# A decoder block on one core: the expert stage gathers its tokens by f32 products from a residual kept in the weights' column order, adds its results into a second buffer, and has four more weight tiles

## The chip, the cores and the metric

One NeuronCore of a Trainium2 chip runs the whole program. The metric is the device time in microseconds of one execution. TensorE (PE) multiplies matrices, with its weight loads (PEld) shown apart; VectorE (DVE), ScalarE (ACT) and GpSimd (POOL) work elementwise; the sync engine (SP) issues the large DMAs, which 16 DMA engines carry out. All engines run side by side and wait for each other by semaphores.

## The reference

A decoder block over 512 tokens of 2048 columns, all in f32: an attention half (two head groups, of which nothing is touched here), the output projection with a residual, and then a mixture of 32 experts in four groups. Cut to what matters:

```python
mix = jnp.concatenate([o_nsa, o_gla], axis=-1)
x = x + g1 * (mix @ w_out[l])
h = _rmsnorm(x, norm2_w[l]) * (1.0 + sc2) + sh2
# group = argmax(h @ w_rg + b_rg); inside it the two experts of the largest logits (h @ w_re + b_re)
# expert e on its tokens xb: (silu(xb @ w_gate[e]) * (xb @ w_up[e])) @ w_down[e], weighted, added up
x = x + g2 * _moe(h, w_rg, b_rg, w_re, b_re, w_gate, w_up, w_down)
return _rmsnorm(x, norm_f_w)
```

Each expert has 12 MB of weights (gate and up 2048 x 512, down 512 x 2048), and all 32 are read once, whichever tokens they get: 403 MB of the 580 MB that the program reads.

## The kernel before, in words

The program is written as one function that records instructions; a scheduling layer puts them on the engines' queues, and makes an instruction wait when a tile's buffer is still read or written by an earlier user. `tc.issue_after` pins an instruction behind another one. A tile name such as `raw` is a ring of buffers: a DMA into the next one waits until its last reader is through.

*Output projection* (loop over n, four column chunks of 512, and q, four groups of rows). `mhi` and `mlo` are the mixer's output, split in two fp32r parts (fp32r is a format whose product takes one pass), held in the buffers `hi0..3` and `lo0..3` of the pool `big`. `wo_products` multiplies; L947 and L948 scale the sum by g1 and add x, which gives the residual `x1`; L950 sums its squares. Transposes of `x1` times `wr2` give the router's logits along the way (L975-978, and for the last chunk L958-969).

*Routing.* The weights of the norm follow as `r2`; `h2_chunk(n)` writes `x1` times `r2` in two fp32r parts, `h2h` and `h2l`, into `hi{n}` and `lo{n}`, with its columns reordered: the experts' gate and up weights are loaded so that a partition p holds four neighbouring rows 4p to 4p+3, and the reordering makes every 128 columns match one of these rows. `WARM` matmuls on TensorE stand ahead of the routing's first counting products (L1057). `onehot` builds `G`, a 0/1 matrix from tokens to the slots of a block of experts.

*Expert stage.* Twelve blocks of 128 slots: the first has experts 0 and 1 (64 slots each); then, sorted by their token count, three experts (64 + 32 + 32) or two (64 + 64) in the order 3, 3, 2, 3, 3, 2, 3, 3, 2, 3, 3. A block's steps, each pinned behind the one before by `then`:

- `gather(n, i)`: for each column chunk n, `G` times `h2h` and `h2l` over four token tiles, eight products into one PSUM bank; ACT copies the bank to `xe`
- `turn(n)`: four transposes of `xe`; ACT scales and shifts them by the second norm into `xt`
- `gate_up(n, which)`: each expert's columns of `xt` times its 1 MB weight tile; experts sit in different column groups of the array and run at the same time
- `weights`, `turn_up`, and `down(hf, kk)`: the scatter matrix, the transposed activation, the down product
- `scatter(n, i)`: the results, split in two, times the scatter matrix, added to `x1` by DVE (L1253)

`run_block` interleaves them: gather n+1 stands between the two halves of `gate_up` of n, the last two chunks of the previous block's scatter between the gathers. `wtile` hands out the weight tiles of 1 MB: four `raw`, three `raw2`, and once, for tiles 8 and 9, two sets of small buffers that are still free (`early`). All weight tiles are issued by SP in this order. The end norms `x1` and stores it.

Of the kernel before, what the change touches and what calls it, by code (L numbers as in the profile page):

```python
# [8 lines left out]
F32 = mybir.dt.float32  # L9
# [22 lines left out]
WARM = 6  # L32
# [6 lines left out]
def block_kernel(ctx, tc, a, out, dbg=None, stop=None):  # L39
# [823 lines left out]
    mp = RS.enter_context(tc.tile_pool(name="mp", bufs=1, side="right"))  # L863
    x1 = x1p.tile([128, NT, D], F32, name="x1")
# [19 lines left out]
    wr2 = mp.tile([128, KT, 36], F32, name="wr2")  # L884
# [16 lines left out]
    for n in range(4):  # L901
# [6 lines left out]
        for q in range(4):  # L908
# [21 lines left out]
            if n == 0 and q == 3:  # L930
                wr = raw_tile([128, KT, 36])
                nc.scalar.dma_start(wr[:, :, 32:36], a["w_router_group"][0].rearrange("(k p) e -> p k e", p=128))
                nc.scalar.dma_start(wr[:, :, 0:32], a["w_router_expert"][0].rearrange("(k p) e -> p k e", p=128))
# [3 lines left out]
                for kt in range(KT):  # L937
                    nc.tensor.matmul(ps[:, 0:36], modc[:, 3, kt:kt + 1].to_broadcast([128, 128]), wr[:, kt],
                                         start=(kt == 0), stop=(kt == KT - 1))
                nc.vector.tensor_add(lgc, lgc, ps[:, 0:36])  # L940
                nc.vector.tensor_tensor(wr2, wr, w2c[:, :, None].to_broadcast([128, KT, 36]), OP.mult)
            for k, i in [(k, i) for k in range(4) for i in range(NT)] if q < 3 else []:
                wo_products(4 * q + k, i, hl[k])
        for i in range(NT):
            for k in range(4):
                wo_products(12 + k, i, hl[k])
            nc.vector.tensor_mul(x1[:, i, cs], pso[i], g1b)  # L947
            nc.vector.tensor_add(x1[:, i, cs], x1[:, i, cs], xr[:, i])  # L948
            jk = mp.tile([128, 512], F32, name="jk", tag="xe", bufs=3)
            nc.scalar.activation(jk, x1[:, i, cs], AF.Square, accum_out=ssp[:, i, n:n + 1])  # L950
            if n == 3:
# [8 lines left out]
                zc = nc.scalar.copy(zT, ps)  # L960
# [23 lines left out]


    h2h, h2l = [None] * 4, [None] * 4

    def h2_chunk(n):
        cs = slice(512 * n, 512 * n + 512)
        h2h[n] = big.tile([128, NT, 512], F32R, name=f"h2h{n}", tag=f"hi{n}")  # L990
        h2l[n] = big.tile([128, NT, 512], F32R, name=f"h2l{n}", tag=f"lo{n}")
        for i in range(NT):
            src = x1[:, i, cs].rearrange("t (p j) -> t j p", j=4)
            hi = h2h[n][:, i].rearrange("t (j p) -> t j p", j=4)
            lo = h2l[n][:, i].rearrange("t (j p) -> t j p", j=4)
            nc.scalar.activation(hi, src, AF.Copy, scale=r2[:, i:i + 1])
            nc.vector.scalar_tensor_tensor(lo, src, r2[:, i:i + 1], hi.bitcast(F32), op0=OP.mult, op1=OP.subtract)

    h2_chunk(0)
# [24 lines left out]
    def onehot(places, cols):  # L1024

        G = mp.tile([128, NT, 128], F32R, name="G", tag="G", bufs=2)
        for c0, cn, s0, sn in cols:
            ins = nc.vector.tensor_tensor(G[:, :, s0:s0 + cn * sn].rearrange("p i (e s) -> p i e s", e=cn),  # L1028
                                          iot[:, None, None, 0:sn].to_broadcast([128, NT, cn, sn]),
                                          places[:, :, c0:c0 + cn, None].to_broadcast([128, NT, cn, sn]), OP.is_equal)  # L1030
        return G, ins
# [38 lines left out]
    G0, g_ins = onehot(pos1, [(0, 2, 0, 64)])  # L1070
# [88 lines left out]

    class Block:  # L1160

        def __init__(self, experts, G, GW, cuts=((0, 512),)):
            self.experts, self.G, self.GW, self.cuts = experts, G, GW, cuts
# [3 lines left out]
            self.xe, self.xt, self.y = {}, {}, {}  # L1169

        def gather(self, n, i):
            if i == 0:
                self.pg = pB("pst")
            nc.tensor.matmul(self.pg, self.G[:, i], h2h[n][:, i], start=(i == 0), stop=False)  # L1174
            ins = nc.tensor.matmul(self.pg, self.G[:, i], h2l[n][:, i], start=False, stop=(i == NT - 1))  # L1175
            if i == NT - 1:
# [332 lines left out]
```

## Time and profile before

| | |
|---|---|
| median of 3 runs | 2138.7 us (2135.83 to 2147.29) |
| the profiled execution | 2135.08 us, span 2133.4 us |
| TensorE busy | 1934.6 us (91%) |
| VectorE busy | 947.4 us (44%) |
| ScalarE busy | 677.0 us (32%) |
| DMA, main queue | 583.05 MB, 74.1% of the 16 engines' time |
| mean granted TensorE clock | 0.984 |

The profile is of one execution. It gives busy times by engine, the span in 40 slices, the DMA's share and rate, groups of instructions by line with the idle time ahead of them, and a timeline. An f32 product stands in it as two records, an fp32r product or a transpose as one. The span of a record on TensorE is modelled and overlaps the next; what a product costs in a row is read from the starts.

### The profile page before, as it was taken

What the parts mean: (1) busy time and instruction counts of PE and PEld (TensorE: products, weight loads), DVE (VectorE), ACT (ScalarE), POOL (GpSimd) and SP (SyncE); (2) the same over time, 40 slices, a digit from 0 to 9 for tenths busy, and PEclk for the clock granted to TensorE, in tenths of its full rate; (3) what the DMA queues carried; (4) which work ended last, traced back from release to release, by engine and by line L of the source; (5) the groups of instructions that cost most, each with busy time, mean ns of one, the idle gap of its engine ahead of it and who ended that gap; (6) DMA issues with size and microseconds to landing.
All of it is one profiled execution on the core that took longest, in us unless ns stands there. A gap on an engine that the chain in (4) does not pass through costs nothing. (4 is left out here: it accounts for less than half of the span.)

```text
span 2133.4 us, 29142 instructions
## 1 busy us (share of the span) xinstructions
PE 1934.6 (91%) x11126; PEld 1129.4 (53%) x11126; DVE 947.4 (44%) x2098; ACT 677.0 (32%) x1443; POOL 57.5 (3%) x112
## 2 busy tenths in 40 slices
PE   6989999999999999999979888997889888998885
PEld 4646777777777787877734332442324323343322
DVE  4667876468764965576352121230212311221205
ACT  4433567466543443323342101111112111111112
POOL 0001000000000000100000000000000000000000
PEclk8999999999999999999989999999999999999998
DMA  8996735326463774676248999999999999999995
GB/s 289 315 296 168 207 107 130 88 63 182 122 183 95 219 207 133 222 268 220 99 186 334 413 403 405 397 401 406 413 394 376 419 404 415 397 390 408 394 414 184
DMA packets 241891, 595.42 MB, mean 279 GB/s; under 512 B 23154, under 2 KB 105272, under 8 KB 208724
## 3 DMA queue, kind: packets, MB, share of 16 engines
q1 hardware_dynamic: 227424, 583.05, 74.1%
q10 hardware_dynamic: 11764, 6.27, 1.1%
q0 software_dynamic: 2560, 4.20, 1.0%
q8 instruction: 89, 1.46, 0.3%
q14 instruction: 54, 0.44, 0.1%
HBM read 580.37 MB, written 7.86 MB: 276 GB/s over the span
## 5 line engine op out<-in xcount | busy, mean ns | idle before, releaser
L1199 PE MATMUL pgu<-raw,xt 128*32 128x512 f32 (+1 forms) x2544 | 404.4, 606 | 64.4 <-DMA raw<-in_w_expert_gate_dram 45.2
L1199 PEld LDWEIGHTS pgu<-raw,xt 128*32 128x32 f32 (+1 forms) x2544 | 110.2, 116 | 323.5 <-issue 199.3
L1234 PE MATMUL pd<-raw,aT 128*32 128x512 f32 (+1 forms) x1280 | 246.4, 598 | 31.8 <-DMA raw<-in_w_expert_down_dram 22.1
L360 PE MATMUL pj<-hthi,wlo 128*128 128x512 f32 (+1 forms) x624 | 250.6, 402 | 4.0 <-DVE wlo L355 3.9
L358 PE MATMUL pj<-hthi,whi 128*128 128x512 f32 (+1 forms) x624 | 251.4, 403 | 0.7 <-ACT a L403 0.7
L359 PE MATMUL pj<-htlo,whi 128*128 128x512 f32 (+1 forms) x624 | 249.6, 400 | 0.5 <-issue 0.5
L1253 DVE TENSOR_TENSOR x<-x,pss 128x512 f32<-128x512 f32 (+1 forms) x196 | 127.1, 674 | 257.8 <-PE pss L1252 257.6
L163 DVE SCALAR_TENSOR_TENSOR acc<-raw,csil,acc 128x512 f32<-128x512 f32 x296 | 222.1, 751 | 27.9 <-DMA raw<-in_w_ada_dram 23.5
L1234 PEld LDWEIGHTS pd<-raw,aT 128*32 128x32 f32 (+1 forms) x1280 | 69.8, 114 | 193.3 <-issue 104.0
L1178 ACT COPY xe<-pst 128x512 f32<-128x512 f32 x48 | 28.1, 585 | 391.8 <-PE pst L1175 391.8
L354 ACT CAST whi<-raw 128x512 fp32r<-128x512 f32 (+1 forms) x156 | 94.9, 614 | 177.0 <-PE pj L359 162.4
L355 DVE TENSOR_TENSOR wlo<-raw,whi 128x512 fp32r<-128x512 f32 (+1 forms) x156 | 105.4, 681 | 88.0 <-ACT whi L354 81.9
L360 PEld LDWEIGHTS pj<-hthi,wlo 128*128 128x128 f32 (+1 forms) x624 | 116.6, 187 | 29.9 <-DVE wlo L355 5.2
L358 PEld LDWEIGHTS pj<-hthi,whi 128*128 128x128 f32 (+1 forms) x624 | 116.7, 187 | 26.5 <-issue 3.6
L359 PEld LDWEIGHTS pj<-htlo,whi 128*128 128x128 f32 (+1 forms) x624 | 116.6, 187 | 26.0 <-issue 4.4
L1243 ACT CAST y<-y 128x512 fp32r<-128x512 f32 (+1 forms) x49 | 29.8, 609 | 295.0 <-DVE y L1241 291.6
L1241 DVE SCALAR_TENSOR_TENSOR y<-pd,ws,g2b 128x512 f32<-128x512 f32 (+1 forms) x49 | 36.1, 737 | 170.8 <-PE pd L1234 170.7
L1251 PE MATMUL pss<-y,T 128*128 128x512 f32 (+1 forms) x196 | 87.4, 446 | 14.7 <-DVE x L1253 14.2
L1188 ACT ACTIVATE xt<-pst,modp,w2p 128x128 f32<-128x128 f32 x192 | 73.5, 457 | 37.6 <-PE pst L1185 37.6
L1174 PE MATMUL pst<-h2h,G 128*128 128x512 f32 x192 | 80.9, 421 | 1.4 <-DVE G L1028 1.2
L606 ACT ACTIVATE s<-s,mx 128x128 f32<-128x128 f32 (+3 forms) x128 | 70.9, 556 | 18.5 <-DVE mx L604 17.9
L1252 PE MATMUL pss<-y,T 128*128 128x512 f32 (+1 forms) x196 | 76.6, 391 | 0.0
(479 smaller groups left out, 2668.8 us busy)
## 6 DMA issues: line engine op xcount, KB each, us to landing
raw<-in_w_expert_down_dram SPq DMA_DIRECT2D x128, 1024.0 KB, 11.8
raw<-in_w_expert_gate_dram SPq DMA_DIRECT2D x127, 1024.0 KB, 11.5
raw<-in_w_expert_up_dram SPq DMA_DIRECT2D x127, 1024.0 KB, 10.1
raw<-in_w_ada_dram SPq DMA_DIRECT2D x96, 1024.0 KB, 6.7
raw<-in_w_in_dram SPq DMA_DIRECT2D x38, 1024.0 KB, 6.1
raw<-in_w_out_dram SPq DMA_DIRECT2D x16, 1024.0 KB, 5.2
raw<-in_x_dram SPq DMA_DIRECT2D x8, 1024.0 KB, 6.2
rkv<-in_w_in_dram SPq DMA_DIRECT2D x4, 1024.0 KB, 9.1
```

What stands on the lines that cost most here:

```text
L163: nc.vector.scalar_tensor_tensor(acc, wt[:, k], csil[:, kt:kt + 1], acc, op0=OP.mult, op1=OP.add)
L354: nc.scalar.copy(hi[:, :, 0:n], src)
L355: nc.vector.tensor_sub(lo[:, :, 0:n], src, hi[:, :, 0:n].bitcast(F32))
L358: nc.tensor.matmul(ps[:n], hi[:, k, 0:n], hthi[kt // 4][:, kt % 4], start=(kt == 0), stop=False)
L359: nc.tensor.matmul(ps[:n], hi[:, k, 0:n], htlo[kt // 4][:, kt % 4], start=False, stop=False)
L360: nc.tensor.matmul(ps[:n], lo[:, k, 0:n], hthi[kt // 4][:, kt % 4], start=False, stop=(kt == KT - 1))
L1174: nc.tensor.matmul(self.pg, self.G[:, i], h2h[n][:, i], start=(i == 0), stop=False)
L1199: ins = nc.tensor.matmul(self.gu[which][s0:s0 + u], self.xt[n][:, k, s0:s0 + u], wts[x][k], start=(n == 0 and k == 0), stop=(n == 3 and k ...
L1234: ins = nc.tensor.matmul(self.pd[c][s0:s0 + u], self.aT[:, 2 * kk + k, s0:s0 + u], wts[x][:, k, 512 * c:512 * c + 512], start=(kk == 0 and ...
L1251: nc.tensor.matmul(ps, self.T[:, 128 * i:128 * i + 128], yh, start=True, stop=False)
L1252: ins = nc.tensor.matmul(ps, self.T[:, 128 * i:128 * i + 128], yl, start=False, stop=True)
L1253: nc.vector.tensor_add(x1[:, i, c0:c0 + cn], x1[:, i, c0:c0 + cn], ps)
```

## The change

The residual `x1` is written with its columns already in the order of the experts' weights (L947 and L948 read their sources strided), so the router's weights `wr` and the per-column vectors are taken in that order too. `h2_chunk` is gone: no `h2h`, `h2l`. `onehot` also makes `GR`, `G` times `r2` by token, and the gather multiplies `x1` itself, as the stationary operand, with `GR`, in f32: the result comes out transposed, so `xe`, its copy and `turn` go too. The scatter adds into `acc`, a second buffer in `hi0..3`; the first block's scatter adds `x1`, read strided back to the plain order, to the result. `lo0..3` become four more weight tiles, `raw3`: eleven in the steady state after seven, and tile 0 moves to the small buffers. `WARM` goes from 6 to 4. The sort of the experts moves behind the next `gate_up`.

```diff
-WARM = 6
+WARM = 4
...
-            nc.vector.tensor_mul(x1[:, i, cs], pso[i], g1b)
-            nc.vector.tensor_add(x1[:, i, cs], x1[:, i, cs], xr[:, i])
+            xq = x1[:, i, cs].rearrange("t (j p) -> t j p", j=4)
+            nc.vector.tensor_mul(xq, pso[i].rearrange("t (p j) -> t j p", j=4), g1b.rearrange("t (p j) -> t j p", j=4))
+            nc.vector.tensor_add(xq, xq, xr[:, i].rearrange("t (p j) -> t j p", j=4))
...
-    def h2_chunk(n):
-        cs = slice(512 * n, 512 * n + 512)
-        h2h[n] = big.tile([128, NT, 512], F32R, name=f"h2h{n}", tag=f"hi{n}")
-        h2l[n] = big.tile([128, NT, 512], F32R, name=f"h2l{n}", tag=f"lo{n}")
-        for i in range(NT):
...
-            nc.scalar.activation(hi, src, AF.Copy, scale=r2[:, i:i + 1])
-            nc.vector.scalar_tensor_tensor(lo, src, r2[:, i:i + 1], hi.bitcast(F32), op0=OP.mult, op1=OP.subtract)
...
-        G = mp.tile([128, NT, 128], F32R, name="G", tag="G", bufs=2)
+        G = mp.tile([128, NT, 128], F32, name="G", tag="G", bufs=1)
...
+        GR = mp.tile([128, NT, 128], F32, name="GR", tag="GR", bufs=2)
+        nc.vector.tensor_tensor(GR, G, r2[:, :, None].to_broadcast([128, NT, 128]), OP.mult)
...
+        at = count[0]
         count[0] += 1
-        early = {8: ("yz",) * 4, 9: ("yz", "T", "aT", "sg")}.get(count[0])
+        early = {0: ("yz",) * 4, 8: ("yz", "T", "aT", "sg")}.get(at)
...
-        if (count[0] - 2 * (count[0] > 9)) % 7 in (2, 4, 6):
-            t = lm.tile([128, 4, 512], F32, name="raw2", bufs=3)
-        else:
-            t = raw_tile([128, 4, 512])
-        return t
+        at = (at - 1 - (at > 8)) % 11
+        if at in (0, 1, 2, 7):
+            return big.tile([128, 4, 512], F32, name="raw3", tag=f"lo{min(at, 3)}")
+        if at > 7:
+            return lm.tile([128, 4, 512], F32, name="raw2", bufs=3)
+        return raw_tile([128, 4, 512])
...
+    acc = [big.tile([128, NT, 512], F32, name=f"acc{n}", tag=f"hi{n}") for n in range(4)]
...
-        def gather(self, n, i):
-            if i == 0:
+        def gather(self, n, j):
+
+            if j == 0:
                 self.pg = pB("pst")
-            nc.tensor.matmul(self.pg, self.G[:, i], h2h[n][:, i], start=(i == 0), stop=False)
-            ins = nc.tensor.matmul(self.pg, self.G[:, i], h2l[n][:, i], start=False, stop=(i == NT - 1))
...
+            ps = self.pg[:, 128 * j:128 * j + 128]
+            for i in range(NT):
+                ins = nc.tensor.matmul(ps, x1[:, i, 512 * n + 128 * j:512 * n + 128 * j + 128], self.GR[:, i],
+                                       start=(i == 0), stop=(i == NT - 1))
+            nc.scalar.activation(self.xt[n][:, j], ps, AF.Identity, scale=w2p[:, n, j:j + 1],
+                                 bias=modp[:, 0, n, j:j + 1])
...
-                nc.vector.tensor_add(x1[:, i, c0:c0 + cn], x1[:, i, c0:c0 + cn], ps)
+                if self.begin:
+                    nc.vector.tensor_tensor(acc[n][:, i].rearrange("t (p j) -> t p j", j=4),
+                                            x1[:, i, 512 * n:512 * n + 512].rearrange("t (j p) -> t p j", j=4),
+                                            ps.rearrange("t (p j) -> t p j", j=4), OP.add)
+                else:
+                    to = acc[n][:, i, c0 - 512 * n:c0 - 512 * n + cn]
+                    nc.vector.tensor_add(to, to, ps)
...
-                then(blk.turn, n + 1)
```

The queues show what moves. TensorE at the end of the routing, before: the first gather of the first block (names are out<-in; `x4` is a count), its transposes, and the start of `gate_up`:

```order
L1174 MATMUL pst<-h2h_9668,G 128x512
L1175 MATMUL pst<-h2l_9669,G 128x512
L1174 MATMUL pst<-h2h_9668,G 128x512
L1175 MATMUL pst<-h2l_9669,G 128x512
L1174 MATMUL pst<-h2h_9668,G 128x512
L1175 MATMUL pst<-h2l_9669,G 128x512
L1174 MATMUL pst<-h2h_9668,G 128x512
L1175 MATMUL pst<-h2l_9669,G 128x512
L1185 MATMUL pst<-ident,xe 128x128 x4
L1199 MATMUL pgu<-raw,xt 64x512
L1199 MATMUL pgu<-raw_9816,xt 64x512
```

TensorE at the same place now, from the counting products' last one on to the second gather:

```order
L1054 MATMUL pt<-onb,Mb 32x32
L1175 MATMUL pst<-GR,x_8150 128x128 x16
L1188 MATMUL pgu<-we,xt 64x512
L1188 MATMUL pgu<-raw_9823,xt 64x512
L1188 MATMUL pgu<-we,xt 64x512
L1188 MATMUL pgu<-raw_9823,xt 64x512
L1188 MATMUL pgu<-we,xt 64x512
L1188 MATMUL pgu<-raw_9823,xt 64x512
L1188 MATMUL pgu<-we,xt 64x512
L1188 MATMUL pgu<-raw_9823,xt 64x512
L1175 MATMUL pst<-GR,x_8150 128x128 x16
```

Eight products and four transposes became sixteen products, and nothing stands between a gather and the products that use it.

SP's queue from the last issue of the output projection's weights on, before. `raw2_10027` is the first tile that has to wait for a tile already read by the experts' products, together with `raw_9938` ahead of it:

```order
L1150 DMA raw_9814<-in_w_expert_gate_dram 128x2048
L1150 DMA raw_9857<-in_w_expert_up_dram 128x2048
L1150 DMA raw_9869<-in_w_expert_gate_dram 128x2048
L1150 DMA raw2_9816<-in_w_expert_gate_dram 128x2048
L1150 DMA raw2_9859<-in_w_expert_up_dram 128x2048
L1150 DMA raw2_9871<-in_w_expert_gate_dram 128x2048
L1150 DMA raw_9912<-in_w_expert_up_dram 128x2048
L1148 DMA we_9933<-in_w_expert_gate_dram 128x512
L1150 DMA raw_9938<-in_w_expert_gate_dram 128x2048
L1150 DMA raw2_10027<-in_w_expert_up_dram 128x2048
```

SP's queue at the same place now; here `raw3_10015` is the first that waits for the experts' products:

```order
L1144 DMA raw_9867<-in_w_expert_gate_dram 128x2048
L1144 DMA raw3_9855<-in_w_expert_up_dram 128x2048
L1144 DMA raw_9869<-in_w_expert_gate_dram 128x2048
L1144 DMA raw3_9857<-in_w_expert_up_dram 128x2048
L1144 DMA raw_9939<-in_w_expert_up_dram 128x2048
L1144 DMA raw3_9959<-in_w_expert_gate_dram 128x2048
L1144 DMA raw_9941<-in_w_expert_up_dram 128x2048
L1144 DMA raw2_10001<-in_w_expert_up_dram 128x2048
L1142 DMA we_9954<-in_w_expert_gate_dram 128x512
L1144 DMA raw2_10003<-in_w_expert_up_dram 128x2048
L1144 DMA raw2_10013<-in_w_expert_gate_dram 128x2048
L1144 DMA raw3_10015<-in_w_expert_gate_dram 128x2048
```

With the two sets of small buffers, whose pieces stand earlier in both queues, nine tiles can be under way ahead of the first that waits for the experts, and now thirteen; `raw3_9823`, one row above this piece, is the first of them. The piece `we` of a small set keeps its place behind the warm-up matmuls, which read its buffer.

More of the change, by code (lines that the diff above doesn't have):

```diff
@@ L883, in block_kernel @@
     lgc = consts.tile([128, 36], F32, name="lgc")
-    wr2 = mp.tile([128, KT, 36], F32, name="wr2")
+    wr2 = mp.tile([128, KT, 36], F32, name="wr2", tag="G", bufs=1)
     def sm(name, shape, dt=F32, tag=None):
@@ L959, in block_kernel @@
                 zT = mp.tile([128, 512], F32, name="zT", tag="xe", bufs=3)
-                zc = nc.scalar.copy(zT, ps)
+                nc.scalar.copy(zT, ps)
                 for j in range(4):
@@ L1271, in run_block @@
             if n < 3:
-                before_gather(blk, n + 1)
+                if n == 1 and blk is first:
+                    with tc.issue_after(at[0].ins):
+                        sort_experts()
                 left = prev is not None and n < 2
-                for i in range(NT):
-                    then(blk.gather, n + 1, i)
-                    if left and i in (0, 2):
-                        then(prev.scatter, 2 + n, i // 2)
-                if left:
-                    then(prev.scatter, 2 + n, 2)
-                    then(prev.scatter, 2 + n, 3)
-                elif n == 2:
+                for j in range(4):
+                    then(blk.gather, n + 1, j)
+                    if left:
+                        then(prev.scatter, 2 + n, j)
+                if n == 2:
                     then(blk.weights)
-                then(blk.turn, n + 1)
             then(blk.gate_up, n, 1)
@@ L1288, in run_block @@
         if nxt is not None:
-            for i in range(NT):
-                then(nxt.gather, 0, i)
+            for j in range(4):
+                then(nxt.gather, 0, j)
         then(blk.turn_up)
-        if nxt is not None:
-            then(nxt.turn, 0)
         then(blk.down, 0, 0)
@@ L1345, in sort_experts @@
             nc.vector.tensor_copy(dst, ps[:, 0:NT * NE].rearrange("p (i e) -> p i e", i=NT))
-    def before_gather(blk, n):
-        if blk is first:
-            with tc.issue_after(g_ins.ins), tc.issue_after(zc.ins):
-                h2_chunk(n)
-                if n == 3:
-                    sort_experts()
     def weighted(G, weights, cols):
@@ L1372, in begin_next @@
         cols = blocks.pop(0)
-        G, _ = onehot(poss, cols)
+        G, GR = onehot(poss, cols)
         experts = [(nc.values_load(ordi[0:1, c:c + 1], engines=[mybir.EngineType.SP], min_val=0, max_val=NE - 1),
                     s0 + sn * (c - c0), sn) for c0, cn, s0, sn in cols for c in range(c0, c0 + cn)]
-        return Block(experts, G, weighted(G, Ws, cols), ((0, 512),) if blocks else ((0, 256), (256, 256)))
+        return Block(experts, GR, weighted(G, Ws, cols), cuts=((0, 512),) if blocks else ((0, 256), (256, 256)))
     blk, prev = first, None
-    for i in range(NT):
-        then(blk.gather, 0, i)
-    then(blk.turn, 0)
+    for j in range(4):
+        then(blk.gather, 0, j)
     while blk is not None:
@@ L1436, in block_kernel @@
         nc.vector.tensor_reduce(we4, tov, axis=AX.X, op=OP.add)
-        G = mp.tile([128, NT, 128], F32R, name="G", tag="G", bufs=2)
+        GR = mp.tile([128, NT, 128], F32, name="GR", tag="GR", bufs=2)
         GW = mp.tile([128, NT, 128], F32, name="GW", tag="xe", bufs=3)
         for i in range(NT):
-            nc.vector.tensor_scalar(G[:, i], iot, sl4[:, i:i + 1], None, op0=OP.is_equal)
-            nc.vector.tensor_scalar(GW[:, i], G[:, i].bitcast(F32), we4[:, i:i + 1], None, op0=OP.mult)
-        blk = Block([(e_reg, 0, 128)], G, GW)
+            nc.vector.tensor_scalar(GR[:, i], iot, sl4[:, i:i + 1], r2[:, i:i + 1], op0=OP.is_equal, op1=OP.mult)
+            nc.vector.tensor_scalar(GW[:, i], iot, sl4[:, i:i + 1], we4[:, i:i + 1], op0=OP.is_equal, op1=OP.mult)
+        blk = Block([(e_reg, 0, 128)], GR, GW)
         for n in range(4):
-            for i in range(NT):
-                blk.gather(n, i)
-            blk.turn(n)
+            for j in range(4):
+                blk.gather(n, j)
             for which in range(2):
```

50 lines of the change are left out of this document (18 added, 32 removed).

## The prediction, made before the changed kernel was run

> **What bounds the kernel now.** I read the slices of the page first, then a table of stages, then the timeline around the start of the expert stage. The slices:
>
> ```profile
> PE   6989999999999999999979888997889888998885
> DMA  8996735326463774676248999999999999999995
> GB/s 289 315 296 168 207 107 130 88 63 182 122 183 95 219 207 133 222 268 220 99 186 334 413 403 405 397 401 406 413 394 376 419 404 415 397 390 408 394 414 184
> ```
>
> One slice is 53 us. In the first twenty TensorE is full and the DMA is not; from slice 22 on it is the other way round. The table of windows (window, length, busy time of each engine with its count, granted clock, DMA share, GB/s) cuts the second half at the points where something changes:
>
> ```profile
> 1074.00:1113.00 39.00, 31.22 (x121) 14.82 (x123) 24.51 (x71) 21.12 (x29) 2.29 (x2) 0.79 0.42 166
> 1113.00:1140.00 27.00, 25.98 (x132) 11.98 (x130) 2.71 (x7) 7.68 (x16) 1.35 (x2) 1.00 0.74 267
> 1140.00:1360.00 220.00, 192.94 (x1104) 74.39 (x1102) 50.46 (x76) 34.24 (x75) 2.50 (x3) 0.99 1.02 408
> 1360.00:1390.00 30.00, 29.71 (x142) 12.73 (x140) 4.02 (x7) 5.50 (x14) 1.35 (x2) 1.00 0.94 360
> ...
> 1610.00:1650.00 40.00, 39.41 (x187) 17.69 (x187) 5.55 (x10) 9.43 (x23) 1.41 (x2) 1.00 0.95 368
> ...
> 1860.00:1900.00 40.00, 39.41 (x187) 17.68 (x186) 5.72 (x10) 9.43 (x23) 1.35 (x2) 1.00 0.96 371
> 1900.00:2096.00 196.00, 167.40 (x964) 61.46 (x964) 39.56 (x60) 25.92 (x58) 1.20 (x2) 0.99 1.01 402
> 2096.00:2134.00 38.00, 17.14 (x77) 9.21 (x71) 22.36 (x41) 12.86 (x35) 1.01 (x1) 0.74 0.35 112
> ```
>
> From 1140 to 2096 the weight stream fills the DMA engines, except in three short stretches inside two-expert blocks where the share falls to 0.94-0.96 and TensorE is the full one. So the end is set by when the stream gets going, by 384 tiles of 1.049 MB at about 408 GB/s (2.57 us each), and by a tail of 38 us. Between 1074 and 1140 it carried 166 x 39 + 267 x 27 = 13.7 MB where 408 GB/s would carry 26.9: 13.2 MB, or 32 us of stream, are missing there. The timeline of the sync engine's DMA issues and of TensorE shows why:
>
> ```profile
> 1086.40 0.33 SPq L1148 DMA_DIRECT2D we<-in_w_expert_gate_dram  x1
> 1088.13 0.48 PE L1174 MATMUL pst<-h2h,G 128*128 128x512 f32 x1 [1.22 <-DVE G L1028]
> ...
> 1089.84 0.40 PE L1175 MATMUL pst<-h2l,G 128*128 128x512 f32 x1
> 1092.12 0.66 PE L1185 MATMUL pst<-ident,xe 128*128 128x128 f32 x4 [1.88 <-ACT xe L1178]
> 1093.32 5.35 PE L1199 MATMUL pgu<-raw,xt 128*64 128x512 f32 x16 [0.55 <-ACT xt L1188]
> 1098.60 0.50 PE L1174 MATMUL pst<-h2h,G 128*128 128x512 f32 x1
> 1098.69 0.33 SPq L1150 DMA_DIRECT2D raw<-in_w_expert_gate_dram  x1
> ...
> 1105.11 1.06 PE L1185 MATMUL pst<-ident,xe 128*128 128x128 f32 x4
> ```
>
> After the ninth tile (1086.40) nothing is issued until the first products free two tiles at 1098.6. Every tile is full and waits to be read.
>
> **The change, part by part.**
>
> *Four more tiles.* Nine tiles can be loaded before the first product; now thirteen: the new ones take the space of `mlo`, read for the last time in the output projection. Three of its four parts come free while the projection still runs, the fourth at its end, and all are filled in idle DMA time before 1093. Each tile moved into idle time leaves the full stretch one tile shorter: 4 x 2.57 = 10.3 us. Bounds: 0 if the lead is lost again inside the first block, 10.3 plus the shortfalls below at best.
>
> *Steady depth 7 to 11 tiles.* The three short stretches lose, by share against 1.015, 2.2 + 2.6 + 2.2 = 7 us, by rate against 408 GB/s 3.5 + 3.9 + 3.6 = 11 us. TensorE is slower in those blocks after the change (next part), so I take 5, bounds 0 and 11.
>
> *The gather.* Before, eight products of 512 columns, 1089.84 + 0.23 - 1088.13 = 1.9 us at the pace of the rows above, then four transposes of about 0.53 to the next instruction: 2.4 us. Now sixteen f32 products 128 x 128 with the residual as the stationary side, two records each. Such a product stands in the program's first stage, in the timeline and the line's own view:
>
> ```profile
> 19.11 6.87 PE L238 MATMUL pt<-dg,raw 128*128 128x128 f32 x56 [0.21 <-ACT xnT L240]
> L238 PEld LDWEIGHTS pt<-dg,raw x128: 185/192/334, 11.1 to 29.2; 128*128 128x128 f32 x128
> L238 PE MATMUL pt<-dg,raw x128: 275/276/580, 11.1 to 29.3; 128*128 128x128 f32 x128
> ```
>
> 56 records in 6.87 us are 123 ns each, though one weight load takes 192: the loads overlap. A gather is then 32 x 0.123 = 3.9 us, 1.5 more. A two-expert block lasts from here to here:
>
> ```profile
> 1350.51 3.65 PE L1199 MATMUL pgu<-raw,xt 128*64 128x512 f32 x16
> ...
> 1416.87 3.64 PE L1199 MATMUL pgu<-raw,xt 128*32 128x512 f32 x32
> ```
>
> 66.4 us, full of work; a three-expert block has the same count of passes, four experts' columns at a time. So a block becomes 72 us of TensorE. Its weights take 24 x 2.57 = 62 us (two experts) or 36 x 2.57 = 93 (three). Over the cycle of 3 + 3 + 2 experts TensorE needs 216 of the stream's 247: the added 6 us per block hide behind the weights, some 70 us in all. In the two-expert block the stream runs 10 us, four tiles, ahead: with two or three tiles being read and two in flight, eleven hold that, seven would not. If this cover were gone, the price is under the rivals.
>
> *First block.* Gone from the way: the copy of `xe`, which waited (1.88), the four transposes and 0.55; in chunk 1 the gather began at 1098.60 and was through 1.9 later, yet its transposes came only at 1105.11, behind the sort's products, which waited for `h2_chunk` on DVE: 4.6 lost. Added: one DVE multiply for `GR` (0.75 by the row of L1241 below) ahead of the first gather, and 1.5 in each of four gathers. Two fewer warm-up matmuls let the counting products start earlier:
>
> ```profile
> 1078.21 8.16 PE L1004 MATMUL sc<-sg,ident 128*128 128x512 f32 x12
> ...
> 1083.27 0.29 DVE L1051 TENSOR_TENSOR Mb<-o,om 128x128 bf16<-128x128 f32 x1
> ...
> 1086.21 0.18 PE L1057 MATMUL pt<-Mb,upb 128*128 128x32 bf16 x1
> ```
>
> `Mb` was ready at 1083.6, and TensorE still had 2.6 us of warm-up to do. Two matmuls are four of the twelve records; at 0.43 each (the block row above: 16 records, two column groups side by side, in 3.65) they end 1.7 us sooner. But they also keep the clock. Windows of 3.41 us, as the clock changes:
>
> ```profile
> 1087.18:1090.59 3.41, 2.10 (x8) 1.43 (x8) 3.18 (x10) 3.40 (x6) 0.00 (x0) 1.00 0.23 77
> 1090.60:1094.00 3.40, 1.34 (x8) 0.76 (x10) 3.40 (x9) 2.65 (x6) 0.00 (x0) 1.00 0.03 5
> 1094.01:1097.42 3.41, 3.41 (x10) 0.98 (x8) 3.41 (x4) 0.30 (x1) 1.74 (x1) 0.50 0.00 0
> ```
>
> A window with 2.10 us of products left the clock full, one with 1.34 was followed by half. After the change the window from 1083.8 holds about 1.3 us (rest of the warm-up, counting, start of the gather), so I charge half clock for one window of the first gather: +1.7, which eats the 1.7. The Trainium skill's "TensorE: Matmul & The Clock Gate" (What's actually happening) gives the same window of 3413 ns but names an idle window as what halves the clock; by that the 1.7 would not be charged. The trace's window was only 60% idle, so I stay with the row. In sum TensorE reaches the first down product some 3-5 us earlier (2.4 from the first chunk, 4.6 and up from the second, less 1.5 to 4.5 for the gathers passed by then). The first scatter then reads x1 strided; the nearest rows for that are these:
>
> ```profile
> L997 DVE SCALAR_TENSOR_TENSOR h2l<-x,r,h2h x16: 1102/1134/1815, 1060.3 to 1101.6; 128x512 fp32r<-128x512 f32 x16
> L1241 DVE SCALAR_TENSOR_TENSOR y<-pd,ws,g2b x49: 478/750/753, 1152.4 to 2105.3; 128x512 f32<-128x512 f32 x47, 128x256 f32<-128x256 f32 x2
> ```
>
> The same operation costs 1.13 strided, 0.75 not: +0.4 for each of sixteen adds, half of which nothing covers (scatters 0 and 1 stand alone, 2 and 3 lie between gathers): +3. Net of the first block: -2, bounds -7 and +3.
>
> *Output projection.* L947 and L948 now also run strided, 2 x 0.4 x 16 = 13 us more on DVE. For n < 3 TensorE hardly waits for them; this is the row of its waits from 840 to 1075 (total, times, longest):
>
> ```profile
> PE pt L975 <- DVE x L948: 0.9, 4, 0.3
> ```
>
> With 0.8 more behind the last tile of each of the three steps that can cost 2.4, if no product of the next step fills it, and they are there to fill it. At n = 3 the strided pair (+0.8) takes the place of one L997 (-1.13) per token tile. I take +1, bounds -2 and +3. Router loads in eight pieces instead of two sit on ACT's queue, which waits for TensorE there: 0. Elsewhere one `GR` multiply per block on a DVE that is idle, and the tail reads `acc` in place of x1: 0.
>
> **Sum.** -10.3 - 5 - 2 + 1 = -16.3, in round numbers -16. The profiled execution took 2135.1 (span 2133.4), 3.6 under the median of 2138.7; 2135.1 - 16 = 2119, as a median 2122.5.
>
> **Rivals.**
>
> *The gather becomes the bound (slower).* Place: the sixteen products per chunk. If the weight loads were not hidden, 32 x 0.192 = 6.1 us, a block is 56.8 + 4 x 6.1 = 81, even with the stream (82 a block on average), two-expert blocks overrun the tiles, and the gain is gone: about 2138. If the 276 ns that one record's span shows set the pace, a gather is 8.8, a block 92, and eleven blocks cost 10 us each over the stream: about 2235. It decides at (82 - 56.8) / 4 / 32 = 0.197 us a record. For it: L238's stretch may profit from an order that this one, mixed with scatters, lacks. Against it: 56 records in a row at 0.123. Chance 0.09.
>
> *The lead is lost in the first block (no change).* TensorE paces the stream up to 1140, and it has more work in this block; if half clock holds for more than one window or the strided adds stall the scatters, the four tiles only make up for it: -3 to -9, 2130 to 2136. For it: 25.98 of 27 us busy in 1113-1140. Against it: 7 us of stalls go (1.88, 0.55 and 4.6). Chance 0.22.
>
> *More transfers in flight raise the rate (faster still).* If eleven tiles lift 402-408 GB/s to the best slice's 419, 850 us shrink by up to 3%: -16 - 5 to -25, 2100 to 2117. Against it: the share is already 1.01. Chance 0.15.
>
> **How the numbers follow.** The forecast's own range is 2115 to 2128, chance 0.50; 0.04 is left for something in the projection stage. 0.5% is 10.7 us, about what a measurement of this kernel can tell from no change. Faster by that: 0.50 + 0.15 + 0.03 of the rest = 0.68; slower: 0.07 of the first rival and 0.01 of the rest; between: 0.22 and what remains, 0.24. The range takes in the faster rival down to 2105 and the no-change one up to 2139.
>
> **What would show it.** In the profile after: thirteen tile issues before the first expert product; DMA over 1074-1140 some 4 MB more; the full stretch starting with more tiles landed and ending about 16 us sooner; gather lines at 0.12 us a record and less of TensorE's time spent waiting for weights; no dip below 1.0 in the two-expert blocks. It is wrong if gather records start over 0.2 us apart, if the sync queue still stalls on TensorE deep in the stage, or if the warm-up products start later than the 1078.21 of before.

## The result: 2159.9 us, slower by 1%

The changed kernel takes 2159.94 us (median of 4 runs, 2159.58 to 2166.11), the kernel before 2138.27 on the same chip: a ratio of 1.0103, interval 1.0085 to 1.0120. The forecast was 2122.5. The slices of the profile after, to be laid beside those of before:

```profile
PE   6989999999999999999988988998989988889885
DMA  8987634225453863676358999999999999999994
GB/s 297 312 280 186 201 108 113 84 86 159 142 166 110 240 195 129 196 266 238 130 192 326 377 401 401 413 364 396 418 396 398 374 393 417 403 395 372 399 406 158
```

The stream comes to its full rate a slice later (377 GB/s in the slice where it had 413 before) and still dips three times (364, 374, 372). The windows, cut as before at 1074, 1113 and 1140, then by blocks (length, busy time of PE, PEld, DVE, ACT, POOL, granted clock, DMA share, GB/s):

```profile
1074.00:1113.00 39.00, 30.26 (x135) 18.64 (x134) 11.12 (x49) 6.56 (x14) 1.59 (x2) 0.74 0.46 169
1113.00:1140.00 27.00, 24.75 (x149) 14.10 (x146) 3.92 (x19) 4.35 (x9) 1.20 (x2) 1.00 0.70 247
1140.00:1361.00 221.00, 194.85 (x1296) 86.41 (x1296) 54.61 (x76) 32.68 (x65) 4.56 (x5) 1.00 0.96 379
1361.00:1438.00 77.00, 71.09 (x361) 34.27 (x360) 18.56 (x30) 11.63 (x24) 1.59 (x2) 1.00 0.99 397
```

With four tiles more to fill, 1074 to 1140 carried no more than before: 169 x 39 + 247 x 27 = 13.3 MB for 13.7. And from 1140 on the share is 0.96 where it was 1.02. The two-expert block lasts 77 us, 66.4 before, 72 forecast. The timeline of TensorE shows why:

```profile
1081.88 6.47 PE L993 MATMUL sc<-sg,ident 128*128 128x512 f32 x8
...
1090.86 2.02 PE L1175 MATMUL pst<-GR,x 128*128 128x128 f32 x8 [1.97 <-DVE w L1078]
1093.48 2.08 PE L1175 MATMUL pst<-GR,x 128*128 128x128 f32 x8 [0.60 <-ACT xt L1177]
...
1106.20 1.16 PE L1175 MATMUL pst<-GR,x 128*128 128x128 f32 x8
1107.90 1.16 PE L1175 MATMUL pst<-GR,x 128*128 128x128 f32 x8 [0.55 <-ACT xt L1177]
1109.61 1.16 PE L1175 MATMUL pst<-GR,x 128*128 128x128 f32 x8 [0.55 <-ACT xt L1177]
1111.32 1.16 PE L1175 MATMUL pst<-GR,x 128*128 128x128 f32 x8 [0.55 <-ACT xt L1177]
1112.40 1.94 PE L1188 MATMUL pgu<-raw,xt 128*64 128x512 f32 x8
```

The second gather takes 1112.40 - 1106.20 = 6.2 us, not 3.9. Its groups of eight records (one `j`) start 1.71 apart: 0.91 of products and 0.8 of waiting, of which the row names 0.55. What ends the wait is ACT's `xt`, L1177: the activation that reads group `j` from a quarter of the PSUM tile (PSUM is the memory for TensorE's results) into whose next quarter TensorE wants to write group `j + 1`. The first gather ran at half clock (2.08 a group) as well and took 9.9; the granted clock is 0.50 from 1090.9 to 1104.4. In the table of waits (total, times, longest):

```profile
PEld pst L1175 <- ACT xt L1177: 91.2, 142, 0.9
```

Three waits in each of 48 gathers would be 144. No row of the kernel before has this wait: there a bank was filled by all its products, and then read.

### The profile page after: what moved, and what is told of

The parts are those of the page before. It is cut to its first block, busy times and chain, and to the rows that moved or that the text cites. A ratio compares the mean times of both kernels' runs of the same rounds, so it can differ in the third digit from the quotient of the medians.

```text
span 2158.3 us, 30930 instructions
## 1 busy us (share of the span) xinstructions
PE 1964.5 (91%) x12082; PEld 1201.9 (56%) x12082; DVE 956.8 (44%) x2094; ACT 648.7 (30%) x1379; POOL 59.1 (3%) x112
## 5 line engine op out<-in xcount | busy, mean ns | idle before, releaser
L1188 PE MATMUL pgu<-raw,xt 128*32 128x512 f32 (+1 forms) x2544 | 361.2, 596 | 16.1 <-DMA raw<-in_w_expert_up_dram 11.3
L1175 PE MATMUL pst<-GR,x 128*128 128x128 f32 x1536 | 226.0, 291 | 49.8 <-ACT xt L1177 42.3
L1175 PEld LDWEIGHTS pst<-GR,x 128*128 128x128 f32 x1536 | 189.1, 194 | 131.0 <-ACT xt L1177 91.2
L1223 PE MATMUL pd<-raw,aT 128*32 128x512 f32 (+1 forms) x1280 | 223.8, 598 | 33.5 <-DMA raw<-in_w_expert_down_dram 13.9
L1248 DVE TENSOR_TENSOR acc<-acc,pss 128x512 f32<-128x512 f32 (+1 forms) x180 | 118.4, 674 | 269.6 <-PE pss L1241 269.0
L1188 PEld LDWEIGHTS pgu<-raw,xt 128*32 128x32 f32 (+1 forms) x2544 | 103.3, 115 | 239.6 <-issue 200.8
L1177 ACT ACTIVATE xt<-pst,modp,w2p 128x128 f32<-128x128 f32 x192 | 87.8, 457 | 492.7 <-PE pst L1175 492.7
L1223 PEld LDWEIGHTS pd<-raw,aT 128*32 128x32 f32 (+1 forms) x1280 | 63.8, 115 | 179.3 <-issue 104.1
L1240 PE MATMUL pss<-y,T 128*128 128x512 f32 (+1 forms) x196 | 92.5, 472 | 15.8 <-DVE acc L1248 13.0
L1201 DVE TENSOR_SCALAR T<-pst 128x512 fp32r<-128x512 f32 x12 | 8.3, 692 | 164.1 <-PE pst L1199 164.1
L1241 PE MATMUL pss<-y,T 128*128 128x512 f32 (+1 forms) x196 | 76.8, 392 | 0.0
```

What stands on the lines that cost most here:

```text
L1175: ins = nc.tensor.matmul(ps, x1[:, i, 512 * n + 128 * j:512 * n + 128 * j + 128], self.GR[:, i], start=(i == 0), stop=(i == NT - 1))
L1177: nc.scalar.activation(self.xt[n][:, j], ps, AF.Identity, scale=w2p[:, n, j:j + 1], bias=modp[:, 0, n, j:j + 1])
L1188: ins = nc.tensor.matmul(self.gu[which][s0:s0 + u], self.xt[n][:, k, s0:s0 + u], wts[x][k], start=(n == 0 and k == 0), stop=(n == 3 and k ...
L1223: ins = nc.tensor.matmul(self.pd[c][s0:s0 + u], self.aT[:, 2 * kk + k, s0:s0 + u], wts[x][:, k, 512 * c:512 * c + 512], start=(kk == 0 and ...
L1240: nc.tensor.matmul(ps, self.T[:, 128 * i:128 * i + 128], yh, start=True, stop=False)
L1248: nc.vector.tensor_add(to, to, ps)
```

## Experiments

The theories are these. A: the wait between the groups of a gather makes the loss. B: the f32 products themselves do. C: the strided DVE work does (L952, L953 behind the output projection, and the first block's adds). E: a deeper queue of transfers slows the stream. F, later: the longer body of the last loop makes the jump over it dearer. Each is timed against runs of the kernel before on the same chip.

### The activations behind all products

```diff
-            nc.scalar.activation(self.xt[n][:, j], ps, AF.Identity, scale=w2p[:, n, j:j + 1],
-                                 bias=modp[:, 0, n, j:j + 1])
+            for jj in range(4 if j == 3 else 0):
+                nc.scalar.activation(self.xt[n][:, jj], self.pg[:, 128 * jj:128 * jj + 128], AF.Identity,
+                                     scale=w2p[:, n, jj:jj + 1], bias=modp[:, 0, n, jj:jj + 1])
```

> The changed kernel with one edit: the four ACT activations of a gather stand behind all sixteen products instead of one behind each four. Theory A (the loss is TensorE's wait, about 0.8 us three times a gather, for ACT's read of a slice of the PSUM tile into which it writes the next slice): a gather that stands alone falls from 6.1 us to about 3.7 (32 records at 0.114), the first one from 9.9 to 6 or less; a two-expert block falls from 78 to about 73 us, the first block begins about 3 us sooner and is some 7 us shorter; the whole falls from 2160 to 2137-2147. Rival B (the f32 products themselves, 0.114 us a record, are the cost and the waits are only where it shows): gather rows of TensorE stay above 5 us and the time within 4 us of 2160. Rival C (the slower end of the projection, +3 us, and the strided adds): 2155-2160, since this edit doesn't touch them.

2131.27 us, 0.9962 of before (0.9948 to 0.9976), 29 us under the changed kernel and better than expected. The gather that stands ahead of `turn_up` in the two-expert block, and the first rows of that block and of the next:

```profile
1348.68 0.65 PE L1189 MATMUL pgu<-raw,xt 128*64 128x512 f32 x2
...
1392.20 3.84 PE L1175 MATMUL pst<-GR,x 128*128 128x128 f32 x32
1395.88 0.60 PE L1211 MATMUL pst<-ident,sg__11445 128*128 128x128 f32 x4
1398.18 8.16 PE L1224 MATMUL pd<-raw,aT 128*64 128x512 f32 x34 [1.70 <-ACT aT L1213]
...
1420.69 0.64 PE L1189 MATMUL pgu<-raw,xt 128*32 128x512 f32 x4
```

32 records in 1395.88 - 1392.20 = 3.68 us, 0.115 each, and a block of 72.0 us. The first block, from its first gate product to the next block's, falls from 82.7 to 73.6 us. A holds; B as the main cause falls. The time is below A's range of 2137-2147.

### Seven weight tiles, with and without the wait

Both give back the `wtile` of the kernel before (nine tiles ahead, a ring of seven); the second has the activations behind the products as well.

```diff
-        at = (at - 1 - (at > 8)) % 11
-        if at in (0, 1, 2, 7):
-            return big.tile([128, 4, 512], F32, name="raw3", tag=f"lo{min(at, 3)}")
-        if at > 7:
-            return lm.tile([128, 4, 512], F32, name="raw2", bufs=3)
-        return raw_tile([128, 4, 512])
+        if (count[0] - 2 * (count[0] > 9)) % 7 in (2, 4, 6):
+            t = lm.tile([128, 4, 512], F32, name="raw2", bufs=3)
+        else:
+            t = raw_tile([128, 4, 512])
+        return t
```

> The changed kernel with the weight tiles of the kernel before (nine tiles ahead, then a ring of seven); gather and column order stay changed. Theory A: the four tiles are worth their 10 us at the start, and more behind it, since TensorE overruns the weights in a two-expert block by 78 - 62 = 16 us, six tiles: 2175-2195. Rival E (a deeper queue of transfers slows the stream, the issue to landing time grew from 11 to 18 us): no slower than 2160, 2145-2160.

> Both edits: the activations behind all sixteen products, and the weight tiles of the kernel before. With the run that has the first edit alone it prices the tiles without the wait. Theory A: the gather then costs 1.3 us more than before and the stalls at its start are gone, so the time stands near the kernel before, 2138-2152, and the four tiles are worth 5 to 12 us. Rival B: 2170-2195, as with seven tiles and the wait.

2214.78 us with the wait (1.0348, 1.0326 to 1.0371), 2167.03 without it (1.0137, 1.0115 to 1.0159): both above the bounds of A, though in its order, and the second nearer to B's 2170. The four tiles are worth 2214.8 - 2159.9 = 55 us with the wait and 2167.0 - 2131.3 = 36 without, where the prediction had 15; E is refuted. The windows of the two-expert block and the one behind it, first without the wait and with seven tiles, then with eleven:

```profile
1351.50:1423.50 72.00, 68.25 (x361) 34.47 (x360) 18.71 (x30) 10.14 (x24) 1.42 (x2) 1.00 0.97 379
1423.50:1516.00 92.50, 79.66 (x556) 35.54 (x558) 18.70 (x29) 10.13 (x24) 1.20 (x1) 0.98 0.99 393
```

```profile
1348.70:1420.70 72.00, 68.25 (x363) 34.47 (x362) 18.70 (x30) 10.14 (x24) 1.42 (x2) 1.00 1.01 412
1420.70:1504.80 84.10, 75.48 (x553) 34.30 (x552) 18.62 (x29) 10.14 (x24) 1.20 (x1) 1.00 1.01 398
```

TensorE's 72 us are the same. With eleven tiles the DMA engines work through them, and the next block finds its weights landed (84.1 us for 92.5); with seven they run dry (0.97), and the next block waits. With seven tiles and the wait the share in the two-expert block falls further:

```profile
1375.50:1452.60 77.10, 71.19 (x361) 34.23 (x360) 18.66 (x30) 11.64 (x24) 1.59 (x2) 1.00 0.88 339
```

So B has a part: with seven tiles and no wait the changed kernel is dearer than the one before by 1.4%, 28 us. The strided DVE work (10 us, below) and the jump at the end (some 3) are in that; the rest, some 15 us by this estimate, is left for the f32 gather, which the deeper ring covers.

### Plain column order, with strided weight loads

The residual stays in the plain order, and the products read it with a stride of four elements.

```diff
-                ins = nc.tensor.matmul(ps, x1[:, i, 512 * n + 128 * j:512 * n + 128 * j + 128], self.GR[:, i],
+                ins = nc.tensor.matmul(ps, x1[:, i, 512 * n:512 * n + 512].rearrange("t (p j) -> t j p", j=4)[:, j], self.GR[:, i],
...
-            nc.vector.tensor_mul(xq, pso[i].rearrange("t (p j) -> t j p", j=4), g1b.rearrange("t (p j) -> t j p", j=4))
-            nc.vector.tensor_add(xq, xq, xr[:, i].rearrange("t (p j) -> t j p", j=4))
+            nc.vector.tensor_mul(x1[:, i, cs], pso[i], g1b)
+            nc.vector.tensor_add(x1[:, i, cs], x1[:, i, cs], xr[:, i])
```

> The activations behind all sixteen products, and the residual in plain column order: the products of the gather read their stationary side with a stride of 16 bytes, the two DVE operations of the projection and the first block's adds run over contiguous columns, the router's loads are the two of before. Against the run with the first edit alone. Rival C (the strided DVE work counts): WARM starts about 2-3 us sooner, the first block's adds take 0.75 us for 1.1, in all 3 to 6 us less. Rival: the weight load of TensorE is slower over a stride: gather records at 0.15 us or more for 0.114, a two-expert block 5 us longer or more, and the time higher than with contiguous columns. If the strided work is covered and the load doesn't mind: within 2 us.

2206.91 us (1.0321, 1.0303 to 1.0339): 76 more than with contiguous loads. The gather's lines (minimum, median, maximum ns):

```profile
L1171 PEld LDWEIGHTS pst<-GR,x x1536: 307/329/333, 1086.2 to 2129.8; 128*128 128x128 f32 x192
L1171 PE MATMUL pst<-GR,x x1536: 271/397/500, 1086.2 to 2129.9; 128*128 128x128 f32 x192
```

A load takes 329 ns for 192, and a gather 7.7 us, 0.24 a record; a two-expert block lasts 88.5 us. This is the case of the rival "the gather becomes the bound": the loads set the pace, 0.24 a record where it put the limit at 0.197. The run without any strided work, below, has the rest of this kernel and is faster than both, so the loss is the loads' alone.

### Two PSUM tiles in turn

The activations are again where the change put them; the groups alternate between two tiles.

```diff
-            if j == 0:
-                self.pg = pB("pst")
+            if j < 2:
+                self.pg = [] if j == 0 else self.pg
+                self.pg.append(pB("pst"))
...
-            ps = self.pg[:, 128 * j:128 * j + 128]
+            ps = self.pg[j % 2][:, 128 * j:128 * j + 128]
```

> The changed kernel, its activations where the change put them (one behind each four products), but the four groups of a gather alternate between two PSUM tiles. Theory A in its narrow form (the wait is for the shared PSUM tile, not for the activation's place in the program): the waits of about 0.8 us between groups go, a gather that stands alone takes 3.7 to 4.2 us, a two-expert block 72 to 73 us, the whole 2128-2137, as with the activations behind all products (2131.3). Rival (an activation between the groups costs TensorE the time whatever tile it reads, or the second tile, now held longer, makes the next step wait): gathers stay above 5 us, or a wait of the same size appears ahead of the next step that needs such a tile: 2145-2160.

2125.52 us, 0.9940 of before (0.9925 to 0.9955), below the range that was expected. The same place as above:

```profile
1386.12 3.84 PE L1177 MATMUL pst<-GR,x 128*128 128x128 f32 x32
1389.80 0.60 PE L1212 MATMUL pst<-ident,sg__11461 128*128 128x128 f32 x4
1391.07 1.51 PE L1225 MATMUL pd<-raw,aT 128*64 128x512 f32 x6 [0.68 <-ACT aT L1214]
```

The wait is gone with the activations in place, so it belongs to the shared tile: A in its narrow form. The Trainium skill says in "PSUM — Partial Sum Buffer", section "PSUM bank collisions raise a hardware error", that two engines have to be kept off one bank by semaphores whatever addresses they touch; 142 waits with one tile and none with two agree with it. The waits in the trace are for semaphores; what would happen without them no run here shows. It is also 6 us better than activations behind the products (2131.1 and 2131.2 in the next two runs, on the same chip). One place is in the rows: there all four stood between the gather and ACT's copy `aT`, and the down products came 2.3 us behind the gather's end (1398.18 - 1395.88); here 1.3. A two-expert block is 71.0 us for 72.0.

### Six warm-up products

```diff
-WARM = 4
+WARM = 6
```

> Activations behind all sixteen products, and six warm-up products instead of four. The prediction charged four of them with one window of half clock (+1.7 us) and credited them with 1.7 us. With the activations moved, the first gather took 4.4 us and the first gate products ran at full clock with four, so there is nothing left to gain: 0 to +2 us against 2131.3, the counting products 1.2 to 1.7 us later. Rival: the two products more keep the clock through the first gather (4.4 to 3.8 us) and the time falls by 1 to 2 us.

Against 2131.27, the run with the same activations and four: 2131.10 us (0.9965, 0.9952 to 0.9977). No difference, as expected. The rival falls as well: from the first gather's start to the first gate product 6.0 us went by with six, 4.4 with four.

### A shorter loop body

```diff
-            for j in range(4):
-                blk.gather(n, j)
+            blk.gather(n, 0)
+            blk.gather(n, 3)
```

> Activations behind all sixteen products; the body of the last loop, which runs no time with this input, holds half of its gather's products (two of four groups a chunk; computation that would only matter if the loop ran is left out). In all kernels with the changed gather TensorE stands 6.3 to 6.9 us at the jump over that loop, 3.6 before. Theory F (the longer body makes the jump dearer): the wait falls to 3.6-5 us, the time by 1 to 3 us. Rival (the wait comes from ACT's or DVE's end, or from where the code lies, not its length): 6.3 or more, time unchanged within 1 us.

2131.22 us (0.9964, 0.9951 to 0.9977), and TensorE's idle time at the jump is 6.73 us. With half of the gather's products gone from the body nothing changes, so F is not borne out.

### No strided work

```diff
-                ins = nc.tensor.matmul(ps, x1[:, i, 512 * n:512 * n + 512].rearrange("t (p j) -> t j p", j=4)[:, j], self.GR[:, i],
+                ins = nc.tensor.matmul(ps, x1[:, i, 512 * n + 128 * j:512 * n + 128 * j + 128], self.GR[:, i],
```

This is the edit against the plain-order kernel. The columns are no longer reordered, so the products pair columns with the wrong weight rows, and the kernel does not compute the block; the instructions, the shapes and the routing stay.

> Activations behind all sixteen products, all DVE work of the residual over contiguous columns (the two operations behind the output projection, the first block's adds), the router's loads as before, and the gather's stationary side contiguous: the reordering of columns inside each 512 is left out. Rival C (strided DVE work costs): from the first product of the projection to the warm-up products 214.5 us as in the run with plain order, against 219.4 to 221.1; the first block 1 us shorter; in all 4 to 8 us less than 2131.3, 2123-2127. If it is covered: 2129-2132. Against the run with plain order, 2206.9, it differs by the stride of the weight loads alone: 75 us or more between them, from 1536 products at about 0.25 against 0.114 us a record.

2121.11 us (0.9917, 0.9903 to 0.9930): 10 us under the kernel with strided DVE work, below the range of 2123-2127, and 86 under the one with strided weight loads. From the latter it differs by that stride alone; from the former also by the router's loads, two for eight pieces, which no run takes apart. The second operation behind the projection, in the changed kernel and here (minimum, median, maximum ns):

```profile
L953 DVE TENSOR_TENSOR x<-x,raw x16: 1053/1066/1110, 905.4 to 1077.4; 128x512 f32<-128x512 f32 x16
```

```profile
L949 DVE TENSOR_TENSOR x<-x,raw x16: 681/691/693, 903.9 to 1071.2; 128x512 f32<-128x512 f32 x16
```

From the projection's first product to the first warm-up product 220.5 us went by in the changed kernel, 215.7 here and 217.4 before. C has its part, then: 10 us, some 5 of them in this stage, beside some 30 of the wait.

### A copy for the gather, written by ACT

Two PSUM tiles; the residual stays plain and is added to in place, as before the change; the gather reads `xp`, which takes the space of `acc`.

```diff
-    acc = [big.tile([128, NT, 512], F32, name=f"acc{n}", tag=f"hi{n}") for n in range(4)]
+    def xp_chunk(n):
+        xp[n] = big.tile([128, NT, 512], F32, name=f"xp{n}", tag=f"hi{n}")
+        for i in range(NT):
+            nc.scalar.copy(xp[n][:, i].rearrange("t (j p) -> t j p", j=4),
+                           x1[:, i, 512 * n:512 * n + 512].rearrange("t (p j) -> t j p", j=4))
...
-                ins = nc.tensor.matmul(ps, x1[:, i, 512 * n + 128 * j:512 * n + 128 * j + 128], self.GR[:, i],
+                ins = nc.tensor.matmul(ps, xp[n][:, i, 128 * j:128 * j + 128], self.GR[:, i],
```

> Two PSUM tiles a gather, eleven weight tiles, and the residual back in plain order: DVE's two operations behind the projection and all adds run over contiguous columns, in place, and the gather reads a second copy in the experts' order, which ACT writes into the space of the changed kernel's result buffer in sixteen strided copies (1.2 us each by ACT's activations of the same form in the kernel before, 19 us in all; half of them before the projection ends, the rest between the first gathers). If ACT has room for them: the 10 us that contiguous work brought (2131.2 to 2121.1) come on top of two tiles a gather (2125.5): 2114-2119. If the copies are late for a gather, or hold up ACT's casts for the projection: 2119-2130.

2117.18 us, 0.9896 of before (0.9879 to 0.9913): the best version, 43 us under the change as it was made. Its copies, and its windows for the first 66 us of the stage:

```profile
L991 ACT COPY xp<-x x16: 1092/1120/1137, 1030.8 to 1098.9; 128x512 f32<-128x512 f32 x16
```

```profile
1074.00:1113.00 39.00, 36.65 (x221) 22.36 (x221) 12.08 (x62) 15.73 (x25) 2.25 (x3) 0.92 0.70 252
1113.00:1140.00 27.00, 25.90 (x160) 14.53 (x158) 2.73 (x5) 8.93 (x17) 1.59 (x2) 1.00 0.87 316
```

252 x 39 + 316 x 27 = 18.4 MB, 4.7 more than before the change: here are the four tiles of the prediction.

### The loop left out

Two PSUM tiles, and no loop.

```diff
-    n_reg = nc.values_load(nov[0:1, 0:1], min_val=0, max_val=40)
-    with tc.For_i(0, n_reg, 1):
...
```

> Two PSUM tiles a gather, and the last loop, which runs no time with this input, left out, so that no engine jumps over it. TensorE then doesn't stand 6.3 to 7.1 us ahead of the last transposes, nor DVE 3.4: by the chain at the end, where the transposes start 3 us behind DVE's reduction, 4 to 7 us less than 2125.5, 2118-2122. Rival (the engines wait for each other's ends there anyway): within 2 us of 2125.5.

2120.66 us (0.9917, 0.9898 to 0.9935), 5 under the kernel with the loop, whose interval overlaps this one. Ahead of its last reduction DVE stands 0.85 us, until ACT's last sum, instead of 3.40 at the jump; and TensorE's transposes are no longer late, since without the loop in their way they are done by 2091, nine microseconds ahead of the reduction:

```profile
2098.99 0.17 DVE L1447 TENSOR_REDUCE ssf<-ssp 128x4 f32<-128x16 f32 x1 [3.40 <-issue]
...
2104.04 8.82 DVE L1463 SCALAR_TENSOR_TENSOR raw<-acc,ssf,nfb 128x512 f32<-128x512 f32 x13 [4.68 <-ACT nfb L1456]
```

```profile
2100.32 0.17 DVE L1408 TENSOR_REDUCE ssf<-ssp 128x4 f32<-128x16 f32 x1 [0.85 <-ACT jk L1401]
...
2101.82 8.70 DVE L1424 SCALAR_TENSOR_TENSOR raw<-acc,ssf,nfb 128x512 f32<-128x512 f32 x13 [1.13 <-POOL ssf L84]
```

The first pair is the kernel with the loop, the second without: 5.05 and 1.50 us from the reduction to the first of the last scalings. From the end of ACT's last sum (2096.40 and 2100.29) it is 7.6 and 1.5, so this chain is 6 us shorter; the two profiled executions are 2.4 us apart.

## Why the prediction was wrong

**The step that failed** is the sentence "A gather is then 32 x 0.123 = 3.9 us". The rate of the records was right (0.115 measured, 3.68 us a gather where nothing waits). Left out was what the diff shows beside it: ACT's activation now stands inside the gather, behind each four products, on the tile that the next four write. I priced the products and never asked which tile the activation reads and who writes it next. It costs 2.5 us in a gather that stands alone (6.2 - 3.7), 5 to 6 us in a two-expert block (77.1 and 78.0 against 72.0) and 9 in the first (82.7 - 73.6). With the wait taken away by a second tile the same change gives 2125.5, 3 us from the forecast of 2122.5 and inside its narrow range, so the wait is 34 of the 37 us of the miss. By place, against the kernel with two tiles: 101.6 us for 87.2 from the warm-up's start to the second block, 848.6 for 826.8 from there to the last block's start.

That the kernel with two tiles comes so near the forecast is in part luck. In its profiled execution, against the one before, the stages ahead of the projection took 2.0 us less, the projection 3.9 more, the first block 1.6 less, the stretch from the second block's start to the last one's 18.0 less, and the last block with the tail 4.8 more: -12.9 in all, for -16.3, with two costs larger than forecast (projection and tail) and the stream's gain larger too.

Point by point, with what each term measured:

- *Four more tiles and steady depth, -10.3 and -5*: the mechanism was right. "eleven hold that, seven would not" is what the two windows show: with a block of 72 us the stream stays at 1.01 with eleven tiles and falls to 0.97 with seven. With 77 to 78 us the overrun is 16 us of weights, six tiles, and eleven don't hold it: the three dips came back. The worth of the tiles, 36 us, is larger than my 15; mine was a difference to the kernel before, with its shorter gather. That the longer gather needs the tiles would explain it, but no run has eleven tiles with the old gather. With two PSUM tiles the stretch from the second block's start to the last one's took 826.8 us, 844.8 before: -18 for -15.
- *"The added 6 us per block hide behind the weights"*: right for 72 us and eleven tiles, wrong for 77. The cover has a limit that I worked out (four tiles) and did not test against a longer gather, though the rival named one of 6.1 us.
- *First block, -2 (-7 to +3)*: with two tiles, from the warm-up's start to the second block's start, 87.2 us for 88.8: -1.6. As the change stands, 101.6: +13, out of the bounds by the waits and by the half clock that came with them (2.08 us a group for 1.16): some 13 us of it in the two kernels with the wait, 3.4 or none in the nine without.
- *Half clock of the first gather, +1.7, and two warm-up products, -1.7*: together nothing, as measured; singly unsettled. With two tiles the first gather took 5.4 us, 1.7 over the 3.7 of a gather at full clock, just as charged; but with four warm-up products it took from 3.7 to 5.4 where no group waited for the next, and 5.4 with six, so the number of warm-up products isn't what decides it.
- *Output projection, +1 (-2 to +3)*: the strided operations took 1.06 us each, 0.4 more than contiguous ones (0.69), as forecast, but the cover I named (products of the next step, "they are there to fill it") is thin: in eight executions with them the stage took 218.4 to 221.3 us, 217.4 before, and 214.4 to 215.7 in the three whose DVE works without stride. Taking all stride away, the first block's adds too, was worth 10 us on the whole. The term was mis-sized by 2 against before, and I did not see that the change could have had -2 there.
- *Tail, 0*: +3. In all ten executions with the changed gather and the loop TensorE stands 6.3 to 7.1 us at the jump over the last loop, ahead of its last transposes, and 3.6 before. First the kernel before, then the one with two tiles:

```profile
2115.32 1.12 PE L1469 MATMUL pst<-ident,colv 128*128 128x128 f32 x4 [3.58 <-issue]
```

```profile
2102.20 1.12 PE L1453 MATMUL pst<-ident,colv 128*128 128x128 f32 x4 [7.07 <-issue]
```

I had not looked there. What makes the difference stays open: it isn't half of the body's gather.

**The rivals.** "The lead is lost in the first block" happened, and worse than its -3: the lead was lost and more. One of its two conditions came true, half clock for more than one window; the wait, which came with it, it didn't name. "The gather becomes the bound" named a gather of 6.1 us, which came true within 0.1 (6.2), by a wait instead of slow loads; but it priced it at 2138, by an even balance over a cycle. The runs show what that left out: the first block, where TensorE sets the stream's pace and every microsecond counts, and a ring that cannot carry the overrun of a two-expert block into the next. "More transfers in flight raise the rate" isn't seen: the windows of the kernel with eleven tiles and no wait have 412 and 398 GB/s, and 402 to 408 stood before. Of the signs set for being wrong, two stood in the profile: groups of eight records 1.71 apart, 0.21 a record, and warm-up products at 1081.88, later than 1078.21. The second says little: the kernel with two tiles starts its warm-up at 1080.15 and gains all the same. The third, the sync queue stalled by TensorE deep in the stage, is no sign at all: it waits there in the kernel before and in the fastest as well.

## What to carry to other kernels

When a step that filled a PSUM tile and then had it read is rewritten so that parts are read while others are still written, look for the reader inside the loop: give neighbouring parts different tiles, or read behind the last product. A queue depth holds an overrun up to so many tiles and none beyond; a step that is "hidden" has a price as soon as it is longer than the depth, and it is worth working out at what length that is. Where a layout must change, put the strided pass on the engine that has time (ACT here), not on the loads of TensorE nor on the path behind a product.

## What the runs showed of the hardware that was not expected

- A stationary operand read with a stride of 16 bytes loads in 329 ns instead of 192, and a gather of 32 records takes 7.7 us for 3.7: 86 us on the whole. DVE's f32 operation with the same stride takes 1.07 for 0.69. The Trainium skill's "SBUF — State Buffer" (section "Door 1: The DMA port swizzle") has lines of 16 bytes and a penalty for each access that goes to a new one; these rows agree, since with this stride every element does; no run here has another stride.
- A jump over a loop that runs no time holds DVE for 3.4 us and TensorE for 3.6 to 7.1; leaving the loop out took 6 us off the chain from ACT's last sum to the last scalings, in part because TensorE's last transposes could then run earlier. The Trainium skill's "Runtime: NRT & Kernel Launch" (section "Instruction fetch mechanics") tells of a stall where a taken branch leaves the fetched pages; the jump's cost is in keeping with that, but no run here shows that fetching is what holds the engines.
